# Moving the modulation column sums behind a step's products, and ordering the later modulation rows behind the convolutions and the gates

## The chip, the cores and the metric

One core of a Trainium2 chip runs the whole block. The metric is the device time of one execution in microseconds (us), smaller is better; the time given for a kernel is the median of its runs. The trace comes from one further, profiled execution.

## The reference

Input is x (1024 tokens by 1024 channels), a conditioning vector c and the weights of one layer. In outline:

```python
mod = silu(c) @ w_mod + b_mod                 # 6 rows of 1024
shift1, scale1, gate1, shift2, scale2, gate2 = split(mod, 6)
h = rms_norm(x, g_norm1) * (1 + scale1) + shift1
x_lru, z_lru, q, k, v = split(h @ w_in)       # 512 channels each
xc = conv4(x_lru) + conv_b                    # depthwise, 4 taps over the tokens
# per direction: r, i = sigmoid(xc @ w_a + b_a), sigmoid(xc @ w_x + b_x)
# a = exp(8 * r * log_sigmoid(lam)); u = sqrt(1 - a*a) * i * xc; h_t = a_t * h_{t-1} + u_t
y_lru = (h_fwd + h_bwd) * gelu(z_lru)
y_att = differential_attention(q, k, v)       # 4 heads, relative bias
x = x + gate1 * (concat(y_lru, y_att) @ w_out)
h2 = rms_norm(x, g_norm2) * (1 + scale2) + shift2
x = x + gate2 * expert_choice_ffn(h2)         # 16 experts, 128 tokens each
```

All matrices are float32. The kernel keeps that precision with split operands: a value is written as hi + lo in a short format, and a product is taken as hi*hi + hi*lo + lo*hi.

## The kernel before

**Stage 1, norm and first projection.** x is normalised, transposed (xT, 8 tiles of 128 channels by 1024 tokens) and turned into h. Tile k of h needs the 128 columns k of scale1 and shift1, so the modulation vector is made in slices: `m_load(k)` loads the weights of slice k in four DMAs, `m_mm(k)` multiplies their first four row blocks (of 8) on TensorE into `mp`, `m_sum(k)` adds the other four on VectorE (three instructions on `mp`, a fourth that writes `acc`), `m_red(k)` sums `acc` over the partitions with two matmuls against a column of ones into `pm`, and `m_col(k)` makes the two columns `acol` and `shc` on VectorE. `h_make(k)` then writes `hh` (ScalarE), the full-precision value (ScalarE again, or VectorE for k in 0, 1, 2, 7) and `hl`, their difference (GpSimd, VectorE for k = 7). `x_mm(k, lo, ms)` are the products of h tile k with the first 256 columns of w_in into the PSUM tiles `px[0]` and `px[1]` (the trace calls them `pjx`): `x_mm(k, False, (m,))` are 4 matmuls of `hh` into `px[m]`, `x_mm(k, True)` are 4 matmuls of `hl`. `w0_split` makes hi and lo of those weights, `lam_table` a small table for the gates.

In this stage the instruction order of TensorE, VectorE and ScalarE is the program's order (a `manual_schedule` block). GpSimd and the DMA queues are ordered by the planner. The loop over k makes slice k + 2 while the products of k and k - 1 run.

**Stage 2, the other projections.** q, k, v, z and the second half of x_lru go through TensorE in 256-column pieces; `do_x(ct, ps)` is the convolution of one 128-channel piece on VectorE (one instruction of line 451, three of line 453, out of PSUM), `do_lru(ct)` the gates (`pg` on TensorE, `tg` on ScalarE, lines 515 and 516 on VectorE, line 521 on GpSimd) and the two scans (lines 523 and 525). `proj_qk` squares and normalises q and k (`sqq`, `rq`, `nq`), transposes them (`pbq`, line 589) and splits them (line 596). Beside that the remaining four modulation rows (gate1, shift2, scale2, gate2) are made in two halves: `mod_rest(half, k)` loads two pieces of 128 x 1024 (`wr`, SyncE's DMA queue, into a ring of five `raw` buffers that the w_in pieces `wi` use too) and adds each to its sum `macc` with one VectorE instruction (line 620). `mod_out(half)` sums `macc` over the partitions on TensorE (`mq`).

In stage 2 a planner lays out every engine's instruction order when the program is built: by its own estimates of costs it takes, for each engine, the earliest instruction of the program that it thinks ready. Each engine then runs its list strictly in that order. `tc.issue_after(i)` keeps the instructions of the block behind i on i's engine. `mod_rest` uses it with the last entry of the list `behind`, to which `proj_qk` appends the instruction that writes `nq` or `nk`.

**After that** attention (about 320 to 556 us of the trace; TensorE, VectorE and ScalarE in program order), routing (556 to 604 us) and the 16 experts (604 to 1166 us), whose weights stream in from HBM.

Of the kernel before, what the change touches and what calls it, by code (L numbers as in the profile page):

```python
# [13 lines left out]
ALU = mybir.AluOpType  # L14
# [7 lines left out]
KT = D // P  # L22
# [34 lines left out]
KS = 3  # L57
KS0 = 1
KLT = 4
# [23 lines left out]
def tile_block(ctx: ExitStack, tc, x, cols, w_mod, b_mod, w_in, wa, wx, lam_qk, relT, w_out, g2, w_router,  # L83
# [68 lines left out]
    def load_in(c0, eng):  # L152
        return [load_half(c0, kk, eng) for kk in range(2)]
# [50 lines left out]
    def lam_table():  # L204
        V.tensor_scalar(out=e2, in0=e1, scalar1=2.0, scalar2=None, op0=ALU.add)
        V.reciprocal(out=e2, in_=e2)
        V.tensor_reduce(out=ls, in_=lp, op=ALU.add, axis=AX.X)
        act(ls, ls, AF.Exp)
        G_.tensor_tensor(out=nlam, in0=ls[:, 1:2], in1=ls[:, 0:1], op=ALU.subtract)
        G_.tensor_scalar(out=nlam, in0=nlam, scalar1=-LAM_INIT, scalar2=None, op0=ALU.add)  # L210
# [123 lines left out]
    def x_mm(k, lo, ms=(0, 1)):  # L334
        for m in ms:
            wh, wl = (w[:, k % 4, m * P:(m + 1) * P] for w in ws0[k // 4])
            for lt, h_ in ((wh, hl[k]),) if lo else ((wh, hh[k]), (wl, hh[k])):
                for n in range(2):
                    mm(px[m][:, n * 512:(n + 1) * 512], lt, h_[:, n * 512:(n + 1) * 512],
                       k == 0 and lt is wh and not lo, k == KT - 1 and lo)  # L340
# [9 lines left out]
    def w0_split(kk, part):  # L350
        if part == 0:
            ws0.append([ylp.tile([P, 4, 256], F32R, tag="y", bufs=NCT, name=f"w0{c}_{kk}") for c in "hl"])
            act(ws0[kk][0], w0r[kk])
        else:
            hi, lo = ws0[kk]
            V.tensor_tensor(out=lo, in0=w0r[kk], in1=hi.bitcast(F32), op=ALU.subtract)
# [14 lines left out]
    with tc.manual_schedule(engines={mybir.EngineType.PE, mybir.EngineType.DVE, mybir.EngineType.Activation}):  # L371
        c_silu()
        tables_a()
        act(rst[:, 0:1], epsc, AF.Sqrt)
        for t in range(NT + 1):
            if t < NT:
                x_stat(t)
            if 1 <= t <= NT:
                if t == NT:
                    m_mm(0)  # L380
                    m_sum(0)
                x_flip(t - 1)
                if t == NT:
                    m_red(0)
            if 2 <= t <= NT:
                x_evac(t - 2)
        w0_split(0, 0)
        m_col(0)
        x_evac(NT - 1, (0,))
        m_mm(1)  # L390
        warm(WU1)
        w0_split(0, 1)
        m_sum(1)
        h_make(0)
        m_red(1)
        m_col(1)
        x_evac(NT - 1, (1,))
        h_make(1)
        x_mm(0, False)
        m_mm(2)  # L400
        m_sum(2)
        x_mm(1, False, (0,))
        m_red(2)
        m_col(2)
        h_make(2)
        for k in range(1, KT + 1):
            if k + 3 < KT:
                m_load(k + 3)
            if k + 2 < KT:
                m_mm(k + 2)  # L410
                m_sum(k + 2)
            if k == 1:
                x_mm(0, True)
            elif k < KT:
                x_mm(k, False, (0,))
            if k + 2 < KT:
                m_red(k + 2)
                m_col(k + 2)
                i_act, i_pv = h_make(k + 2)
                if k + 2 < KT - 1:  # L420
                    i_pool = i_pv
                else:
                    i_dve = i_pv
            if k == KS:
                w0_split(1, 1)
            if k == KLT:
                lam_table()
            if k < KT:
                x_mm(k, False, (1,))
            if 1 < k < KT:  # L430
                x_mm(k - 1, True)
            if k == KS0:
                w0_split(1, 0)
            if k + 2 in (KW, KW + 1):
                wq0.append(load_half(1024, k + 2 - KW, V))
        x_mm(KT - 1, True)
# [11 lines left out]
    def do_x(ct, ps):  # L448
        cw = [col[:, C_CW + 4 * j + ct:C_CW + 4 * j + ct + 1] for j in range(4)]
        xc = lt_(f"xc{ct}")  # L450
        V.tensor_scalar(out=xc, in0=ps, scalar1=cw[2], scalar2=col[:, C_CB + ct:C_CB + ct + 1], op0=ALU.mult, op1=ALU.add)
        for j, o, i in ((0, slice(2, S), slice(0, S - 2)), (1, slice(1, S), slice(0, S - 1)), (3, slice(0, S - 1), slice(1, S))):
            last = V.scalar_tensor_tensor(out=xc[:, o], in0=ps[:, i], scalar=cw[j], in1=xc[:, o], op0=ALU.mult, op1=ALU.add)
        xc_[ct] = xc
        return last
# [21 lines left out]
    def proj_ch(ws, m, name, tag="pj"):  # L477
        ps = psb.tile([P, 1024], F32, tag=tag, bufs=2, name=name)
        for k in range(KT):
            wh, wl = (w[:, k % 4, m * P:(m + 1) * P] for w in ws[k // 4])  # L480
            for lt, hs in ((wh, (hh, hl)), (wl, (hh,))):
                for h_ in hs:
                    for n in range(2):
                        last = k == KT - 1 and lt is wl
                        mm(ps[:, n * 512:(n + 1) * 512], lt, h_[k][:, n * 512:(n + 1) * 512],
                           k == 0 and lt is wh and h_ is hh, last)
        return ps

    y_lru = []

    def do_lru(ct):
        xc = xc_[ct]
        xh = lt_(f"xch{ct}", None, F32R)
        xl = lt_(f"xcl{ct}", None, F32R)
        split(xc, xh, xl, V if ct in LV else G_)
        hs, st = [], []
        for d in range(2):
            pre = []
            for gi in range(2):
                pg = psb.tile([P, 1024], F32, tag="pg", bufs=2, name=f"pg{ct}_{d}_{gi}")  # L500
                i = d * 4 + ct
                for wi_, (w_, xv) in enumerate(((bdh, xh), (bdl, xh), (bdh, xl))):
                    for n in range(2):
                        mm(pg[:, n * 512:(n + 1) * 512], w_[gi][:, i, :], xv[:, n * 512:(n + 1) * 512], wi_ == 0, wi_ == 2)
                tg = lt_(f"tg{ct}_{d}_{gi}")
                act(tg, pg, AF.Tanh, scale=0.5, bias=hb[:, gi * 8 + i:gi * 8 + i + 1])
                pre.append(tg)
            ta, ti = pre
            i = d * 4 + ct
            tt = lt_(f"tt{ct}_{d}")  # L510
            act(tt, ta, AF.Tanh, scale=nkap[:, i:i + 1], bias=nkap[:, i:i + 1])
            act(ta, ta, AF.Exp, scale=kap[:, i:i + 1], bias=kap[:, i:i + 1])
            sq = lt_(f"sqa{ct}_{d}")
            act(sq, ta, AF.Square)
            V.scalar_tensor_tensor(out=tt, in0=sq, scalar=1.0, in1=tt, op0=ALU.add, op1=ALU.mult)
            V.scalar_tensor_tensor(out=ti, in0=ti, scalar=1.0, in1=xc, op0=ALU.add, op1=ALU.mult)
            st.append((ta, ti, tt))
        for d in range(2):
            ta, ti, tt = st[d]
            act(tt, tt, AF.Sqrt, scale=0.25)  # L520
            G_.tensor_tensor(out=ti, in0=ti, in1=tt, op=ALU.mult)
            if d == 0:
                V.tensor_tensor_scan(out=tt, data0=ta, data1=ti, initial=0.0, op0=ALU.mult, op1=ALU.add)
            else:
                V.tensor_tensor_scan(out=tt[:, ::-1], data0=ta[:, ::-1], data1=ti[:, ::-1], initial=0.0,
                                     op0=ALU.mult, op1=ALU.add)
            hs.append(tt)
        V.tensor_tensor(out=hs[0], in0=hs[0], in1=hs[1], op=ALU.add)
        hs_[ct] = hs[0]
# [84 lines left out]
    def mod_rest(half, *ks):  # L614
        for k in ks:
            for i in (2 * half, 2 * half + 1):
                w = raw_tile(f"wr{k}_{i}", [P, 1024])
                SY.dma_start(out=w, in_=w_mod[k * P:(k + 1) * P, (2 + i) * 1024:(3 + i) * 1024])
                with tc.issue_after(behind[-1].ins):
                    V.scalar_tensor_tensor(out=macc[i], in0=w, scalar=sc[:, k:k + 1], in1=macc[i], op0=ALU.mult, op1=ALU.add)  # L620
# [59 lines left out]
        V.tensor_scalar(out=s2w, in0=pw_[:, 0:NE], scalar1=-1.0, scalar2=None, op0=ALU.mult)  # L680

    wv0 = load_in(2048, G_)
    for m in range(2):
        do_x(2 + m, proj_ch(wx1, m, f"pjx1_{m}"))
    mod_rest(1, 2, 3)
    vt = [v_tile(f"v{h}", [P, NT, P]) for h in range(NH)]
    wz1 = load_in(768, V)
    mod_rest(1, 4)
    proj_v(wv0, 0, vt[0:2], lambda _: do_lru(2), VA)
    mod_rest(1, 5, 6)  # L690
    wv1 = load_in(2304, G_)
    do_lru(3)
    mod_rest(1, 7)
# [782 lines left out]
```

## Time and profile before

| | |
|---|---|
| median of 3 runs | 1175.16 us (1174.55, 1175.16, 1177.92) |
| profiled execution | 1174.46 us |
| its span, first to last instruction | 1172.7 us (1.76 us lie around it) |
| mean granted TensorE clock | 0.981 of full speed |
| TensorE busy | 1112.9 us, 95% of the span |
| VectorE, ScalarE, GpSimd busy | 956.9, 795.2, 452.8 us |

An engine's idle time counts for the result only where nothing else covers it. A row of a timeline gives start and duration in us, engine, line, operation, output<-inputs, shape and count of instructions merged into the row, and in brackets the engine's idle time just before it with what ended it. Line 93 is the helper that issues every matmul and line 90 the one that issues every ScalarE instruction, so those are told apart by their tiles.

### The profile page before, as it was taken

How to read it: one execution, taken by the hardware profiler on the slowest of the kernel's cores; microseconds unless marked ns; L12 is line 12 of the kernel's file. 1: busy time of each engine (PE TensorE's matmuls, PEld its weight loads, DVE VectorE, ACT ScalarE, POOL GpSimd, SP SyncE). 2: the span in 40 equal slices, each digit the busy share in tenths (PEclk: the TensorE clock that was granted, in tenths of full speed). 3: DMA queues.
4: the chain of work that ended last, by engine and by line, in shares of the span. 5: the costliest groups of instructions: out<-in, count | busy, mean ns of one | idle time of the engine just before them, and what ended most of it. 6: DMA issues, size and time to landing. Idle time of an engine off the chain costs nothing.

```text
span 1172.7 us, 17849 instructions
## 1 busy us (share of the span) xinstructions
PE 1112.9 (95%) x6303; PEld 933.0 (80%) x6303; DVE 956.9 (82%) x1258; ACT 795.2 (68%) x1051; POOL 452.8 (39%) x528
## 2 busy tenths in 40 slices
PE   5799999899999999999469999999999999999996
PEld 4599998788999998777348888888888888888885
DVE  7576757876498986645779999999999999999995
ACT  7439383186387887433438888888887787888784
POOL 4573332133134454444644323444332444332400
PEclk9899999999999999999779999999999999999998
DMA  9744646613683416336789999999999999999911
GB/s 329 221 126 142 225 135 216 233 55 80 179 246 114 112 37 214 137 127 216 285 326 334 372 394 383 393 389 401 387 394 391 365 391 410 394 392 390 389 39 18
DMA packets 146992, 304.33 MB, mean 260 GB/s; under 512 B 16972, under 2 KB 43724, under 8 KB 146900
## 3 DMA queue, kind: packets, MB, share of 16 engines
q1 hardware_dynamic: 135008, 279.99, 66.0%
q0 software_dynamic: 5488, 19.45, 6.3%
q10 hardware_dynamic: 6408, 3.77, 1.1%
q8 instruction: 49, 0.80, 0.3%
q14 instruction: 39, 0.32, 0.1%
HBM read 277.95 MB, written 25.21 MB: 259 GB/s over the span
## 4 chain that ended last, share of the span: by engine, by line
PE 84%; DVE 6%; DMA 4%; issue 3%; SPq 1%; ACT 1%; POOL 0%; POOLq 0%; DVEq 0%; ACTq 0%
PE ab L93 28%; PE y L93 14%; PE mix L93 7%; PE pv L93 5%; PE sc L93 5%; PE pjk L93 4%; PE pjq L93 3%; PE pjv L93 3%; PE pjz L93 3%; PE pw L815 2%; PE pg L93 2%; PE pjx L93 1%; PE pf L1360 1%; DMA wr<-in_w_mod_dram 1%; PE pe L1269 1%
## 5 line engine op out<-in xcount | busy, mean ns | idle before, releaser
L1260 POOL TENSOR_SCALAR oh<-iot,slot 128x128 bf16<-128x128 bf16 x120 | 143.8, 1213 | 252.6 <-PE pf L1360 238.5
L93 PE MATMUL ab<-wh,xeh 128*128 128x512 f32 x512 | 202.2, 395 | 0.2 <-ACT xeh L90 0.2
L93 PE MATMUL ab<-wh,xel 128*128 128x512 f32 x512 | 199.8, 390 | 0.1
L93 PE MATMUL ab<-wl,xeh 128*128 128x512 f32 x512 | 157.9, 390 | 0.0
L93 PEld LDWEIGHTS ab<-wl,xeh 128*128 128x128 f32 x512 | 96.2, 188 | 20.3
L93 PEld LDWEIGHTS ab<-wh,xel 128*128 128x128 f32 x512 | 96.3, 188 | 19.4 <-DVE xel L1273 0.5
L93 PEld LDWEIGHTS ab<-wh,xeh 128*128 128x128 f32 x512 | 96.1, 188 | 19.3 <-ACT xeh L90 0.5
L142 DVE TENSOR_TENSOR wl<-w_0r,wh 128x1024 fp32r<-128x1024 f32 x79 | 96.8, 1226 | 10.6 <-ACT wh L90 0.4
L90 ACT ACTIVATE wh<-w_0r 128x1024 fp32r<-128x1024 f32 x81 | 85.9, 1062 | 24.6 <-PE ab L93 14.9
L142 DVE TENSOR_TENSOR wl<-w_3r,wh 128x1024 fp32r<-128x1024 f32 x79 | 96.7, 1224 | 6.3
L90 ACT ACTIVATE wh<-w_1r 128x1024 fp32r<-128x1024 f32 x79 | 83.7, 1059 | 22.9 <-PE ab L93 18.2
L90 ACT ACTIVATE wh<-w_3r 128x1024 fp32r<-128x1024 f32 x79 | 83.9, 1062 | 22.3 <-PE ab L93 17.8
L142 DVE TENSOR_TENSOR wl<-w_2r,wh 128x1024 fp32r<-128x1024 f32 x80 | 96.4, 1221 | 2.3 <-ACT wh L90 0.3
L90 ACT ACTIVATE wh<-w_2r 128x1024 fp32r<-128x1024 f32 x80 | 84.9, 1061 | 19.6 <-PE ab L93 18.9
L142 DVE TENSOR_TENSOR wl<-w_1r,wh 128x1024 fp32r<-128x1024 f32 x78 | 92.6, 1220 | 3.6 <-ACT wh L90 1.6
L769 DVE CUSTOM_DVE_ANT_0 p<-sc,bias 128x1024 f32<-128x1024 f32 x64 | 77.8, 1218 | 10.9 <-PE sc L93 10.9
L93 PE MATMUL y<-wh,htl 128*128 128x512 f32 x256 | 83.0, 396 | 0.0
L93 PE MATMUL y<-wh,hth 128*128 128x512 f32 x256 | 81.1, 396 | 0.0
L93 PE MATMUL y<-wl,hth 128*128 128x512 f32 x256 | 79.6, 391 | 0.0
L90 ACT ACTIVATE p<-p,stat 128x1024 f32<-128x1024 f32 x60 | 68.4, 1150 | 0.3 <-DVE stat L769 0.3
L93 PEld LDWEIGHTS pv<-v,wt 128*128 128x128 f32 x512 | 61.7, 192 | 2.5
L93 PE MATMUL pv<-v,wt 128*128 128x128 f32 x512 | 62.1, 275 | 0.0
(466 smaller groups left out, 2832.1 us busy)
## 6 DMA issues: line engine op xcount, KB each, us to landing
w_0r<-in_w_dram SPq DMA_DIRECT2D x81, 512.0 KB, 6.8
w_1r<-in_w_dram SPq DMA_DIRECT2D x79, 512.0 KB, 8.4
w_2r<-in_w_dram SPq DMA_DIRECT2D x78, 512.0 KB, 9.3
w_3r<-in_w_dram SPq DMA_DIRECT2D x77, 512.0 KB, 9.2
wr<-in_w_mod_dram SPq DMA_DIRECT2D x32, 512.0 KB, 4.8
wi<-in_w_in_dram SPq DMA_DIRECT2D x18, 512.0 KB, 4.5
w_5r<-in_w_dram SPq DMA_DIRECT2D x17, 512.0 KB, 8.4
wm<-in_w_mod_dram SPq DMA_DIRECT2D x32, 256.0 KB, 4.9
```

What stands on the lines that cost most here:

```text
L90: return A.activation(out=out, in_=in_, func=func, **kw)
L93: return T.matmul(out, lhsT=lhsT, rhs=rhs, start=start, stop=stop)
L142: return (eng or V).tensor_tensor(out=lo, in0=src, in1=hi.bitcast(F32), op=ALU.subtract)
L769: V.tensor_tensor_reduce(out=p_, in0=scp[g, j], in1=prs[h][0][:, b0:b0 + S], op0=ALU.add, op1=ALU.min, scale=1.0, scalar=3.0e38, accum_out ...
L815: T.transpose(pw[:, b * P:(b + 1) * P], pt_[g, 0][:, kt * P:(kt + 1) * P], ident)
L1260: G_.tensor_scalar(out=oh[:, t, :], in0=iot, scalar1=slot[:, e, t:t + 1], scalar2=None, op0=ALU.is_equal)
L1269: T.transpose(pt[:, b * P:(b + 1) * P], xe[:, (kq * 4 + b) * P:(kq * 4 + b + 1) * P], ident)
L1360: T.transpose(pt[:, b * P:(b + 1) * P], sa[:, b * P:(b + 1) * P], ident)
```

## The change

First, in the loop of stage 1, the block with `m_red(k + 2)`, `m_col(k + 2)` and `h_make(k + 2)` moves from between the two halves of the `hh` products to behind all products of the step; `w0_split(1, 1)` (one VectorE instruction, at k = 3) and `lam_table()` (at k = 4) now stand in front of it. Second, `do_x` and the gate instruction of line 516 leave handles, and the `behind` list gets new last entries, so that the second half's row 4 is queued behind the convolution of piece 2, row 5 behind the convolution of piece 3, and rows 6 and 7 behind the last gate instruction of line 516 in `do_lru(2)`. Rows 0 to 3 stay behind the last `nk`.

```diff
@@ stage 1, loop over k
             elif k < KT:
                 x_mm(k, False, (0,))
+            if k == KS:
+                w0_split(1, 1)
+            if k == KLT:
+                lam_table()
+            if k < KT:
+                x_mm(k, False, (1,))
+            if 1 < k < KT:
+                x_mm(k - 1, True)
             if k + 2 < KT:
                 m_red(k + 2)
                 m_col(k + 2)
...
-            if k == KS:
-                w0_split(1, 1)
-            if k == KLT:
-                lam_table()
-            if k < KT:
-                x_mm(k, False, (1,))
-            if 1 < k < KT:
-                x_mm(k - 1, True)
@@ do_lru
-            V.scalar_tensor_tensor(out=ti, in0=ti, scalar=1.0, in1=xc, op0=ALU.add, op1=ALU.mult)
+            tis.append(V.scalar_tensor_tensor(out=ti, in0=ti, scalar=1.0, in1=xc, op0=ALU.add, op1=ALU.mult))
@@ stage 2
+    convs = []
     for m in range(2):
-        do_x(2 + m, proj_ch(wx1, m, f"pjx1_{m}"))
+        convs.append(do_x(2 + m, proj_ch(wx1, m, f"pjx1_{m}")))
     mod_rest(1, 2, 3)
+    behind.append(convs[0])
     vt = [v_tile(f"v{h}", [P, NT, P]) for h in range(NH)]
     wz1 = load_in(768, V)
     mod_rest(1, 4)
+    behind.append(convs[1])
     proj_v(wv0, 0, vt[0:2], lambda _: do_lru(2), VA)
-    mod_rest(1, 5, 6)
+    mod_rest(1, 5)
+    behind.append(tis[-1])
+    mod_rest(1, 6)
     wv1 = load_in(2304, G_)
     do_lru(3)
     mod_rest(1, 7)
```

## Rows read from the trace of the kernel before

**Rows 1.** The page's first part: busy time, share of the span and instructions of each engine.

```profile
PE 1112.9 (95%) x6303; PEld 933.0 (80%) x6303; DVE 956.9 (82%) x1258; ACT 795.2 (68%) x1051; POOL 452.8 (39%) x528
```

**Rows 2.** Busy time by stretch (start:end and length, then busy us and instructions of PE, PEld, DVE, ACT, POOL, then granted clock, DMA share and GB/s): stage 1 and the experts.

```profile
0.00:66.00 66.00, 48.02 (x281) 34.25 (x282) 41.09 (x86) 38.63 (x58) 37.38 (x89) 0.95 0.83 265
...
604.00:1166.00 562.00, 558.59 (x2672) 457.08 (x2672) 532.95 (x540) 447.60 (x478) 201.34 (x149) 1.00 0.95 352
```

**Rows 3.** What TensorE waited for from 0 to 330 us: us in total, times, longest.

```profile
PE pm L93 <- DVE acc L305: 6.5, 6, 1.6
PE pg L93 <- DVE lk L596: 2.3, 1, 2.3
...
PE pjv L93 <- DVE xc L453: 1.7, 1, 1.7
```

**Rows 4.** TensorE's timeline in stage 1, from the sum of slice 2 to that of slice 6.

```profile
30.39 0.61 PE L93 MATMUL pm<-ones,acc 128*128 128x1 f32 x4 [1.54 <-DVE acc L305]
...
34.32 0.61 PE L93 MATMUL pm<-ones,acc 128*128 128x1 f32 x4 [1.63 <-DVE acc L305]
34.79 0.70 PE L93 MATMUL pjx<-hh,w0h 128*128 128x512 f32 x2
...
35.89 0.85 PE L93 MATMUL mp<-wm,scz 128*32 128x256 f32 x8
36.67 1.22 PE L93 MATMUL pjx<-hh,w0h 128*128 128x512 f32 x2
...
38.90 1.01 PE L93 MATMUL pm<-ones,acc 128*128 128x1 f32 x4 [0.16 <-DVE acc L305]
...
43.28 0.64 PE L93 MATMUL mp<-wm,scz 128*32 128x256 f32 x8
...
46.11 0.61 PE L93 MATMUL pm<-ones,acc 128*128 128x1 f32 x4 [1.04 <-DVE acc L305]
46.57 0.72 PE L93 MATMUL pjx<-hh,w0h 128*128 128x512 f32 x2
...
47.60 1.09 PE L93 MATMUL pjx<-hl,w0h 128*128 128x512 f32 x4
48.61 0.64 PE L93 MATMUL mp<-wm,scz 128*32 128x256 f32 x8
...
51.43 0.61 PE L93 MATMUL pm<-ones,acc 128*128 128x1 f32 x4 [1.05 <-DVE acc L305]
```

**Rows 5.** Busy time by stretch again (columns as in rows 2), for two stretches of stage 1; the figure after the busy times is the granted clock.

```profile
37.00:40.00 3.00, 2.84 (x9) 1.93 (x9) 1.79 (x5) 1.75 (x2) 2.12 (x1) 0.50 1.13 333
...
43.40:57.00 13.60, 10.46 (x63) 6.38 (x61) 7.99 (x20) 6.46 (x6) 6.21 (x3) 1.00 0.44 133
```

**Rows 6.** Timelines of VectorE, ScalarE and GpSimd in stage 1: the sum of slice 5, the weight split, and the tile that `h_make(6)` makes.

```profile
43.99 1.54 DVE L305 SCALAR_TENSOR_TENSOR mp<-wm,sc,mp 128x256 f32<-128x256 f32 x3 [3.76 <-PE mp L93]
45.57 0.48 DVE L305 SCALAR_TENSOR_TENSOR acc<-wm,sc,mp 128x256 f32<-128x256 f32 x1
...
46.95 1.22 DVE L356 TENSOR_TENSOR w0l<-w,w0h 128x1024 fp32r<-128x1024 f32 x1
...
52.40 1.24 ACT L90 ACTIVATE hh<-xT,shc,acol 128x1024 fp32r<-128x1024 f32 x1 [2.81 <-DVE shc L317]
53.67 1.24 ACT L90 ACTIVATE xT<-xT,shc,acol 128x1024 f32<-128x1024 f32 x1
...
54.99 2.36 POOL L329 TENSOR_TENSOR hl<-xT,hh 128x1024 fp32r<-128x1024 f32 x1 [2.96 <-ACT xT L90]
```

**Rows 7.** Timelines of ScalarE, VectorE and TensorE around the first transpose of stage 2.

```profile
80.31 1.06 ACT L90 ACTIVATE bdh<-bd 128x1024 fp32r<-128x1024 f32 x1 [1.26 <-DMA bd<-in_wx_dram]
81.27 1.01 ACT L90 ACTIVATE sqq<-pjq 128x1024 f32<-128x1024 f32 x1
...
84.29 1.23 DVE L582 TENSOR_TENSOR nq<-pjq,rq 128x1024 f32<-128x1024 f32 x1
...
85.66 1.04 PE L589 MATMUL pbq<-ident,nq 128*128 128x128 f32 x8
```

**Rows 8.** Timelines of GpSimd and VectorE around the convolutions of pieces 2 and 3 and the first scan of `do_lru(2)`.

```profile
217.68 2.40 POOL L142 TENSOR_TENSOR wi_1l<-wi,wi_1h 128x1024 fp32r<-128x1024 f32 x1 [11.92 <-ACT wi_1h L90]
...
216.00 1.28 DVE L620 SCALAR_TENSOR_TENSOR macc<-wr,sc,macc 128x1024 f32<-128x1024 f32 x1 [3.11 <-DMA wr<-in_w_mod_dram]
...
218.40 2.77 DVE L620 SCALAR_TENSOR_TENSOR macc<-wr,sc,macc 128x1024 f32<-128x1024 f32 x1
...
233.27 1.27 DVE L596 SCALAR_TENSOR_TENSOR lk<-pbk,gqk,hk 128x1024 fp32r<-128x1024 f32 x1
...
250.22 2.29 DVE L523 TENSOR_TENSOR_SCAN tt<-tg,tg 128x1024 f32<-128x1024 f32 x1 [4.76 <-POOL tg L521]
```

**Rows 9.** All instructions on the modulation sums `macc`: count, shortest/median/longest in ns, and when the first and the last started.

```profile
L620 DVE SCALAR_TENSOR_TENSOR macc<-wr,sc,macc x32: 1267/1278/3266, 75.0 to 241.0; 128x1024 f32<-128x1024 f32 x32
...
L93 PE MATMUL mq<-macc,ones x16: 592/604/617, 188.2 to 270.6; 128*32 128x512 f32 x16
```

**Rows 10.** DMA issues from 0 to 330 us: queue, count, size of one, median us from issue to landing.

```profile
wr<-in_w_mod_dram SPq DMA_DIRECT2D x32, 512.0 KB, 4.8
...
wm<-in_w_mod_dram SPq DMA_DIRECT2D x32, 256.0 KB, 4.9
```

**Rows 11.** SyncE's DMA queue: the issues of the weights of slices 4 to 7, first to last merged.

```profile
26.14 13.64 SPq L288 DMA_DIRECT2D wm<-in_w_mod_dram  x16
```

More of the change, by code (lines that the diff above doesn't have):

```diff
@@ L487, in proj_ch @@
         return ps
-    y_lru = []
+    y_lru, tis = [], []
     def do_lru(ct):
```

## Prediction

> **What bounds the kernel now.** I read the page first. TensorE is busy for 95% of the span [rows 1], so time comes off only where TensorE stands idle or runs at a lower clock. Busy time by stretch says where that is: 48.0 of 66 us in stage 1, against 558.6 of 562 us in the experts [rows 2]. The list of TensorE's waits in the first 330 us names what it stood for: 6.5 us in six waits for `acc`, the modulation sum that VectorE hands to `m_red`, then 2.3 us behind `lk` and 1.7 us behind a convolution [rows 3]. The timeline shows the six waits one by one, each in front of a `pm` matmul [rows 4], and a second granted-clock table shows one more loss: from about 37 us the clock is at 0.50, the lower of its two levels (1.2 instead of 2.4 GHz), and by 43.4 it is back at 1.00 [rows 5]. The clock fell after TensorE had stood idle for 1.54 and then 1.63 us [rows 4].
>
> All sums below go against the profiled execution, 1174.46 us (span 1172.7). The median of the runs shown stands 0.7 above it, and I add that at the end. A difference under 0.3%, 3.5 us, can't be told from no change.
>
> **Part one: `m_red` behind the step's products.** Nothing is added or removed; the same matmuls stand in another order. So the gain is what the waits and the low clock cost.
>
> *Slice 3 (k = 1).* The wait is 1.63 us. The four products from 34.79 to 35.89, 1.10 us, now run in it [rows 4]. VectorE's sum is no earlier, so 0.53 us of wait is left: gain 1.10.
>
> *Slices 4 to 7 (k = 2 to 5).* Twelve matmuls now stand between `m_mm` and `m_red`. Four take 1.03 us (46.57 to 47.60) or 1.01 (47.60 to 48.61) [rows 4], so together about 3.07. VectorE's sum takes 2.06 (43.99 to 45.57 + 0.48) [rows 6]. It is hidden with 1.0 to spare, and the waits of 0.16, 1.04 and 1.05 go, and with them the one for slice 7, about 1.1 (the 6.5 less the five shown). That is 3.3; the first wait of 1.54, for slice 2, stands ahead of the loop and stays [rows 3, 4].
>
> *The clock.* From 36.67 to 43.28 TensorE did twelve products and one `pm` in 6.61 us, 0.16 of it idle [rows 4]. At the high level the same takes 1.03 + 1.03 + 1.01 + 0.46 (`pm`, 46.11 to 46.57) = 3.5, so 2.9 was lost, and 0.2 more on the `mp` group at 35.89 (0.85 against 0.64): 3.1. Does the fall go away? Bounds: 0 and 3.1. It fell behind idle times of 1.54 and 1.63 us; from 43.4 to 57 it stays at 1.00 with single waits of about 1.05 [rows 4, 5]. After the change 1.54 and 0.53 are left, which is neither case. I take 3.1, since the product groups move into the very wait that the fall came behind, and keep 0 as a rival.
>
> *What becomes late.* `h_make(k + 2)` comes three product groups later within the step. For slice 6 `m_red` began at 51.43 [rows 4], `hh` was written from 52.40 to 53.64 and `hl` by 57.35 [rows 6], so 2.2 and 5.9 us behind `m_red`. The first product that reads `hh` stands a whole step later: about 0.46 + 0.57 + 3.07 + 0.46 + 0.57 = 5.1 us (0.57 for an `mp` group: its 0.64 [rows 4] less the overlap with the next). Spare: 2.9; for `hl`, used one step later still, over 5. `w0_split(1, 1)`, 1.22 us [rows 6], and `lam_table`'s small instructions now fall into VectorE's spare microsecond and the 0.46 of `m_red`; if they overrun, they eat from the 2.9. ScalarE is idle for 2.81 us in front of `h_make` [rows 6], which covers the table load that comes forward. Cost: nothing. The weight DMAs hold too: the last of slices 4 to 7 is issued at 39.78 and lands 4.9 us later, about 44.7 [rows 10, 11], while the last `m_mm` would come near 47.1 (34.8 plus three steps of 0.46 + 0.57 + 3.07).
>
> *What follows it into stage 2.* By this sum TensorE ends stage 1 earlier by 1.10 + 3.3 + 3.1 = 7.5 us. Not everything moves with it. `m_red(6)` moves from 51.43 [rows 4] to 34.32 + 3 x 4.1 = 46.6 (a step is 0.46 + 0.57 + 3.07), by 4.8 only, since two product groups that stood behind it now stand in front. GpSimd's `hl` of slice 6 follows it, then the gate tables, the zeroing of the gate weights' tiles and their DMAs, and at last ScalarE's `bdh`, behind which `sqq` is queued; `sqq` leads through `nq` (ends 85.52) to the transposes at 85.66 [rows 7]. There is 0.1 us of spare, so if the order stays, TensorE waits there for the difference: 7.5 - 4.8 - 0.1 = 2.6. If the planner now puts `sqq` in front of `bdh`, the loss is 0. I take 2.6, since the row shows the order as it is. Part one: 7.5 - 2.6 = 4.9.
>
> **Part two: rows 4 to 7 behind convolutions and gates.** No instruction is added. On VectorE a row-4 instruction stood in front of the convolution's second step and held it while its own DMA was in flight: 3.11 us idle, then 1.28; the next took 2.77 [rows 8]. The convolution of piece 2 therefore ended late, its PSUM tile came free late, and TensorE's first `pjv` waited 1.7. Row 5 and 6 instructions then pushed `lk` to 233.27, whose PSUM tile the gates needed: 2.3 [rows 3, 8]. With the rows behind the convolutions, that of piece 2 ends at least 3.11 + 1.28 + 2.77 = 7.2 us earlier, more than the waits behind it, and both should go: 4.0. Bounds: 0, where something else holds the same two tiles, and 4.0. The row instructions behind the waits are the cause named, so I take 4.0.
>
> What is late next: rows 6 and 7, four instructions of 1.28 [rows 9], come after the gates. VectorE is idle for 4.76 us in front of the scan at 250.22 [rows 8], which covers them. Their `raw` buffers come free later, so row 7's two DMAs are issued later on SyncE's queue, behind them on that queue the first loads of attention. The last `macc` instruction began at 241.0, and the `mq` matmuls that read it run at 270 [rows 9]: some 27 us of room for one DMA of 4.8 [rows 10] and 5 us of VectorE.
>
> **Sum.** 1174.46 - 1.10 - 3.3 - 3.1 + 2.6 - 1.7 - 2.3 = 1165.6; with the 0.7 for the median, 1166.3. Attention, routing and experts should only shift: they start when stage 2's tiles are there, and their loads follow their own buffers.
>
> **Rivals.**
>
> *The clock falls all the same.* The 1.54 us wait remains and 0.53 behind it. For: it is the same pair of waits that came before the fall [rows 4]. Against: two thirds of the second are filled. 3.1 less: 1169.4. Chance 0.22.
>
> *GpSimd and VectorE hold each other up.* The `macc` instruction at 218.40 took 2.77 instead of 1.28 while GpSimd ran a 2.40 us subtraction from 217.68; it ended 1.09 after GpSimd did [rows 8]; the longest took 3.27 [rows 9]. Rows 6 and 7 now meet GpSimd's 2.4 us products and splits of `do_lru(2)` and `(3)`. Four times 3.27 - 1.28 is 8 us, of which the 4.76 idle covers a part; the 3 us beyond it and GpSimd's own delay can reach TensorE's gates. Then part two's 4.0 is lost and up to 2 more: 1170.3 to 1172.3, say 1171. Chance 0.12. This is what the Trainium skill states (SBUF — State Buffer, section "SBUF: two separate sides"): a VectorE instruction with two SBUF inputs and a GpSimd instruction that reads SBUF contend for one shared port pair, whoever starts first holds it for the whole instruction, and the other blocks. By that rule the trace agrees, 1.49 us late at 218.40, and these four moved rows are the ones exposed.
>
> *The planner's new order brings new waits.* Stage 2 isn't ordered by hand, and a stage 1 that is shorter by some us changes what it thinks ready. Waits of 1.7 to 2.3 us are what such misplacements cost here [rows 3]; three or four new ones give back 7: 1173. Chance 0.10.
>
> *Slower: row 7 holds VectorE.* If row 7's instructions are queued ahead of the scans, each stands for its DMA as at 216.00: 4.8 + 1.3 us, twice, 12 us, and scans, gates and `mq` behind it stand too. It decides once TensorE loses more than the 8.9 gained and 3.5 beyond; with all 12 and a further stall of 3 or more at `mq`: 1181. Against: the 27 us of room. Chance 0.06.
>
> **How the numbers follow.** Forecast 0.50, the rivals 0.22, 0.12, 0.10 and 0.06. The likeliest case by itself spans 1163.7 (no wait at the transposes) to 1168. Below 1161.5 would need both that and a further wait removed; above 1172.5 lie the last rival and half of the one before. Range 1161.5 to 1172.5. Faster by over 0.3% (below 1171.6) takes in the forecast, the first rival and two thirds of the second: 0.80. Slower (above 1178.7): 0.07, the last rival and a worse case of the third. Same: 0.13.
>
> **What would show it.** Right: the four waits of `pm` for `acc` in the loop gone and one near 0.5 left; the clock at 1.00 through 34 to 45 us; stage 1's last `pjx` 7 us earlier; the first `pbq` waiting about 2.6; no wait of `pjv` for `xc` or of `pg` for `lk`, no VectorE idle behind a `wr` DMA inside a convolution. Wrong: a low clock after the first wait, `macc` instructions above 2 us beside GpSimd near the scans, VectorE idle for a `wr` DMA behind the gates, or waits of TensorE in stage 2 under names that the rows here don't have.

## The result, and the profile after

The changed kernel takes 1164.78 us (median of 6 runs, 1162.60 to 1167.24) against 1175.16 (6 runs, 1171.86 to 1178.21): a ratio of 0.9909, interval 0.9886 to 0.9931. Its profiled execution is the longest of its six, 1167.24 us (span 1165.5, mean granted clock 0.978), so the rows below go against that time and not against the median. A second profiled execution of the same kernel took 1163.18 us (span 1161.5, 0.982); it stands among the experiments as `e11_change`.

The page's first part and the busy time by stretch (columns as in rows 2; the experts now start 7.4 us earlier):

```profile
PE 1113.3 (96%) x6303; PEld 935.2 (80%) x6303; DVE 960.6 (82%) x1258; ACT 795.1 (68%) x1051; POOL 457.9 (39%) x528
```

```profile
0.00:66.00 66.00, 52.35 (x321) 40.54 (x321) 47.14 (x89) 38.54 (x58) 40.23 (x87) 0.92 0.85 272
596.70:1158.70 562.00, 558.54 (x2672) 456.70 (x2672) 533.21 (x540) 447.65 (x477) 202.19 (x149) 1.00 0.95 352
```

TensorE is busy for 52.4 instead of 48.0 us of the first 66 [rows 2]. Of what is left idle there, 11.3 us are waits for the first tiles of x; before it was 11.2, a line that stands above those quoted in [rows 3], and the change doesn't touch it. The experts are the same to 0.05 us. They only shifted: their first matmul started at 604.11 before and starts at 596.75 now, the last one at 1162.36 and 1154.94.

What TensorE waited for from 25 to 330 us (us in total, times, longest):

```profile
PE pg L93 <- ACT tg L90: 2.2, 1, 2.2
PE pm L93 <- DVE acc L305: 2.0, 2, 1.5
PE pbk L589 <- DVE nk L582: 1.2, 1, 1.2
```

Against [rows 3]: the six waits for `acc` are two, and the waits for `lk` and for the convolution are gone. The first line isn't new: it was 1.7 before, below the lines quoted in [rows 3], and is now 2.2. No wait of `pbq` is there.

TensorE's timeline in stage 1, to be laid beside [rows 4]:

```profile
30.25 0.61 PE L93 MATMUL pm<-ones,acc 128*128 128x1 f32 x4 [1.53 <-DVE acc L305]
...
35.03 1.01 PE L93 MATMUL pm<-ones,acc 128*128 128x1 f32 x4 [0.46 <-DVE acc L305]
...
42.27 0.52 PE L93 MATMUL pm<-ones,acc 128*128 128x1 f32 x4
...
46.17 0.50 PE L93 MATMUL pm<-ones,acc 128*128 128x1 f32 x4
...
50.03 0.50 PE L93 MATMUL pm<-ones,acc 128*128 128x1 f32 x4
```

Slices 4 to 7 have no wait. Full-clock steps are 3.86 to 3.90 us long (42.27, 46.17, 50.03), against 5.32 before (46.11 to 51.43, [rows 4]). The step from 35.03 to 42.27 is 7.24: TensorE runs at the lower clock there, as the busy time by stretch shows (the 0.50 behind the busy times is the granted clock).

```profile
28.00:32.00 4.00, 2.47 (x19) 1.47 (x18) 3.16 (x8) 0.78 (x1) 2.33 (x2) 1.00 1.07 322
32.00:42.30 10.30, 9.84 (x32) 6.75 (x31) 5.10 (x11) 3.89 (x4) 5.20 (x3) 0.50 1.13 342
...
253.60:257.40 3.80, 3.73 (x9) 2.94 (x10) 3.80 (x3) 3.73 (x5) 1.00 (x1) 0.55 0.02 4
```

So the clock fell for 10.3 us in stage 1, longer than the 6 to 7 us of before [rows 4, 5], and once more near 254, behind the 2.2 us wait of `pg`.

To compare kernels I use two lengths from TensorE's timeline. **Stage 1** runs from the start of the last matmul of `pt` (the transposes of x) to the first `pjq`, **stage 2** from there to the first `sc` of attention. The clock is the mean granted one of the stretches 28 to 45 us and 230 to 262 us. One profiled execution each:

| kernel | median us | ratio to before, interval | stage 1 | stage 2 | clock 28–45 | clock 230–262 |
|---|---|---|---|---|---|---|
| before | 1175.16 | | 43.37 | 237.41 | 0.80 | 1.00 |
| the change | 1164.78 | 0.9909 (0.9886–0.9931) | 38.72 | 234.99 | 0.70 | 0.95 |
| e11_change, again | 1163.72 | 0.9901 (0.9885–0.9918) | 35.45 | 233.40 | 0.90 | 1.00 |
| e1_stage1_only | 1166.28 | 0.9936 (0.9921–0.9952) | 35.02 | 237.44 | 1.00 | 1.00 |
| e2_rows_only | 1171.45 | 0.9979 (0.9969–0.9990) | 43.73 | 233.40 | 0.80 | 1.00 |
| e3_fill | 1163.42 | 0.9910 (0.9894–0.9925) | 35.50 | 233.40 | 1.00 | 1.00 |
| e4_before_fill | 1174.02 | 0.9990 (0.9981–1.0000) | 42.46 | 238.73 | 1.00 | 0.95 |
| e5_kh | 1161.73 | 0.9888 (0.9869–0.9908) | 33.52 | 233.44 | 1.00 | 1.00 |
| e6_lv | 1163.47 | 0.9905 (0.9885–0.9924) | 34.89 | 232.76 | 1.00 | 1.00 |
| e7_no_gates | 1164.18 | 0.9902 (0.9882–0.9921) | 37.05 | 232.88 | 0.90 | 1.00 |
| e8_conv0_only | 1164.38 | 0.9906 (0.9885–0.9927) | 38.72 | 235.09 | 0.70 | 0.95 |
| e9_kh_lv | 1162.43 | 0.9886 (0.9870–0.9903) | 33.50 | 234.31 | 1.00 | 0.95 |
| e10_kh_lv_nogates | 1159.32 | 0.9862 (0.9846–0.9879) | 33.49 | 231.14 | 1.00 | 1.00 |

The two stages account for the profiled difference: 4.65 + 2.42 = 7.1 of 1174.46 - 1167.24 = 7.2 us. In the second profiled execution they give 7.92 + 4.01 = 11.9, from which 0.7 goes because its last `pt` started that much later (22.84 instead of 22.14): 11.2 of 11.3.

### The profile page after: what moved, and what is told of

Read it like the earlier page. It is cut to its first block, busy times and chain, and to the rows that moved or that the text cites. A ratio compares the mean times of both kernels' runs of the same rounds, so it can differ in the third digit from the quotient of the medians.

```text
span 1165.5 us, 17852 instructions
## 1 busy us (share of the span) xinstructions
PE 1113.3 (96%) x6303; PEld 935.2 (80%) x6303; DVE 960.6 (82%) x1258; ACT 795.1 (68%) x1051; POOL 457.9 (39%) x528
## 4 chain that ended last, share of the span: by engine, by line
PE 88%; DVE 4%; issue 3%; SPq 2%; DMA 1%; ACT 1%; POOLq 0%; POOL 0%; DVEq 0%; ACTq 0%
PE ab L93 28%; PE y L93 14%; PE mix L93 7%; PE pv L93 5%; PE sc L93 5%; PE pjk L93 4%; PE pjv L93 4%; PE pjz L93 4%; PE pjx L93 4%; PE pjq L93 3%; PE pw L820 2%; PE pg L93 2%; SPq L288 1%; PE pf L1365 1%; PE pe L1274 1%
```

## The experiments

**Each part alone.** `e1_stage1_only` has the new loop and the old order of the rows; `e2_rows_only` the old loop and the new order. Against the changed kernel and the kernel before:

```diff
@@ e1_stage1_only, from the changed kernel
-    behind.append(convs[0])
-    behind.append(convs[1])
-    behind.append(tis[-1])
@@ e2_rows_only, from the kernel before
+    behind.append(convs[0])
+    behind.append(convs[1])
+    behind.append(tis[-1])
```

> Only the first part of the change (column sums behind the step's products); rows 4 to 7 as in the kernel before. If the waits count one by one: 4.4 us of waits gone, 0 to 3.1 for the clock, so 1167.7 to 1170.8 against 1175.2; the waits of pjv for the convolution (1.7) and of pg for lk (2.3) still there. Rival, a shift that stage 2 takes back at its first transposes (2.6 us): 1170 to 1173, with a wait in front of pbq.

> Only the second part (rows 4 to 7 behind convolutions and gates); stage 1 as in the kernel before. If the waits count one by one: the waits of 1.7 and 2.3 gone, 4.0 us, so 1171.2; if the row instructions that now stand among the scans cost the gates as much, 1173 to 1175. The six waits for acc in stage 1 (6.5 us) remain. If the two parts add up, the gains of the two runs come to the 10.4 us of the whole change.

TensorE's waits in `e1_stage1_only` (columns as above), and the two `pm` rows of its timeline:

```profile
PE pm L93 <- DVE acc L305: 2.7, 2, 1.5
PE pg L93 <- DVE lk L596: 2.4, 1, 2.4
PE pg L93 <- ACT tg L90: 1.7, 1, 1.7
PE pjv L93 <- DVE xc L453: 1.7, 1, 1.7
```

```profile
30.98 0.61 PE L93 MATMUL pm<-ones,acc 128*128 128x1 f32 x4 [1.54 <-DVE acc L305]
...
35.36 0.61 PE L93 MATMUL pm<-ones,acc 128*128 128x1 f32 x4 [1.16 <-DVE acc L305]
```

The first part alone leaves both waits of stage 2 and takes 8.35 us off stage 1 (43.37 to 35.02) in an execution whose clock didn't fall. Its median of 1166.28 lies 1.4 below the range that I expected for it. There is no wait at `pbq`, with the rows in their old order too. The second part alone takes 4.0 off stage 2 (237.41 to 233.40) and leaves stage 1 within 0.4 us of what it was (43.73 against 43.37), though its waits for `acc` came to 7.9 us instead of 6.5. The parts add up: 0.64% and 0.21% by the ratios, 0.85%, against 0.91% and 0.99% for the whole.

**Is it the idle time that lets the clock fall?** `e3_fill` and `e4_before_fill` put products that nobody reads in front of `m_red`, so that TensorE works through the wait: 6 and 2 of them in front of slices 2 and 3 of the changed kernel; 6, 7, none, 4, 4 and 4 in front of slices 2 to 7 of the kernel before. The edit of `e3_fill`; `e4_before_fill` has other counts:

```diff
+    def fill(n, name):
+        if n:
+            dm = psb.tile([P, 512], F32, tag="pg", bufs=2, name=f"fill{name}")
+            for _ in range(n):
+                mm(dm, ws0[0][0][:, 0, 0:P], hh[0][:, 0:512], True, True)
...
+        fill(6, 2)
         m_red(2)
...
+                fill({1: 2}.get(k, 0), k + 2)
                 m_red(k + 2)
```

> The whole change, and in stage 1's two remaining waits for acc six and two extra 512-column products into a PSUM tile that nobody reads. If the clock falls because TensorE stands idle in these waits: granted clock 1.00 from 28 to 43 us in the profile, and 3.4 to 5.1 us of low clock saved against a run in which it falls, so 1160 to 1162. Rival, a fall that has nothing to do with those waits: the clock still at 0.50 somewhere in 30 to 43 us and 1164.8 as the change itself.

> The kernel before, with the waits of 1.54, 1.63, 1.04, 1.05 and 1.05 us filled with 6, 7, 4, 4 and 4 such products. The waits cost what they cost before, only as busy time; so the time moves by the clock term alone: 1172 (3.1 less) if the fall goes away, 1175 if it does not, and up to 1 us more where the extra products delay the sums.

In both the granted clock stayed at 1.00 from 28 to 45 us, and neither got faster for it: `e3_fill` 1163.42, above the 1160 to 1162 that I expected and not to be told from the change; `e4_before_fill` 1174.02, a ratio of 0.9990, where I expected 1172. In the first, the wait in front of slice 3 was 1.14 us in spite of its fillers:

```profile
30.65 0.58 PE L93 MATMUL pm<-ones,acc 128*128 128x1 f32 x4 [0.26 <-DVE acc L305]
...
35.45 0.58 PE L93 MATMUL pm<-ones,acc 128*128 128x1 f32 x4 [1.14 <-DVE acc L305]
```

In the second, idle time was turned into work (6.5 us of waits became 3.0) that nobody needed, and a 3.4 us stretch of low clock came later, from 234.3 to 237.7:

```profile
234.30:237.70 3.40, 3.25 (x8) 2.57 (x9) 3.40 (x4) 0.28 (x1) 0.00 (x0) 0.51 0.87 321
```

So fillers don't pay. Whether they keep the clock up, one execution of each can't show: `e1_stage1_only` and `e6_lv` run the changed kernel's stage 1 without them and were at 1.00 as well. The thirteen profiled executions together point that way. In eight of them slice 2 waited its full 1.53 to 1.54 us, and in six of the eight the clock fell in stage 1; in the five in which that wait was filled or shorter (0.26 in the two filled ones, 1.05 to 1.06 in `e5_kh`, `e9_kh_lv` and `e10_kh_lv_nogates` below) it fell in none.

**What holds slice 3?** With the clock up, `pm` of slice 3 waits 1.0 to 1.6 us in kernels with the new loop. VectorE's and GpSimd's timelines show why, before (first two lines) and in the changed kernel (last two). `h` is VectorE's full-precision copy, `hl` GpSimd's subtraction:

```profile
31.36 0.94 DVE L326 TENSOR_SCALAR h<-xT,acol,shc 128x1024 f32<-128x1024 f32 x1
...
31.72 5.14 POOL L329 TENSOR_TENSOR hl<-h,hh 128x1024 fp32r<-128x1024 f32 x2
```

```profile
31.22 1.79 DVE L326 TENSOR_SCALAR h<-xT,acol,shc 128x1024 f32<-128x1024 f32 x1
...
30.08 2.37 POOL L329 TENSOR_TENSOR hl<-h,hh 128x1024 fp32r<-128x1024 f32 x1
```

In the profiled execution of the kernel before, VectorE's copy started (31.36) ahead of `hl` and took 0.94. In that of the change GpSimd's `hl` starts first, at 30.08, and ends at 32.45; the copy, begun at 31.22, ends at 33.01, 0.56 behind it. The same copy takes 0.81 where GpSimd is idle. The sum of slice 3 is queued behind the copy.

But it isn't the change that reversed the two. `e2_rows_only` has the old loop, and there GpSimd comes first as well: the copy takes 1.73, and the wait of slice 3 is 2.13 instead of 1.63. On GpSimd a small instruction stands in front of `hl`, `lp` of line 370. In the kernel before it waited for its DMA until 31.30, just ahead of the copy (first line); in `e2_rows_only` it ran 1.60 us ahead of the copy (the other three lines: GpSimd, VectorE, TensorE):

```profile
31.30 0.46 POOL L370 TENSOR_TENSOR lp<-lq 128x128 f32<-128x128 f32 x1 [3.48 <-DMA lq<-in_lam_qk_dram]
...
30.56 0.46 POOL L370 TENSOR_TENSOR lp<-lq 128x128 f32<-128x128 f32 x1 [1.94 <-DMA lq<-in_lam_qk_dram]
...
32.16 1.73 DVE L326 TENSOR_SCALAR h<-xT,acol,shc 128x1024 f32<-128x1024 f32 x1
...
35.91 1.01 PE L93 MATMUL pm<-ones,acc 128*128 128x1 f32 x4 [2.13 <-DVE acc L305]
```

In all nine other profiled executions with this copy on VectorE, old loop or new, `lp` starts 1.4 to 2.1 us ahead of the copy and the copy takes 1.26 to 1.91. The profiled execution that the prediction was read from is the exception. `e5_kh` gives this copy and the one before it to ScalarE, which in the changed kernel was idle for 4.54 us in front of its `hh` at 31.22:

```diff
-KH = (0, 1, 2, 7)
+KH = (0, 7)
```

> The whole change, and the full-precision h tiles of k = 1 and 2 written by ScalarE instead of VectorE. If stage 1's last two waits (1.53 in front of slice 2's sum, 0.46 to 1.16 in front of slice 3's) are VectorE's, held by GpSimd's subtraction of hl on the way (its copy took 2.19 and 1.79 instead of 0.81): the second wait gone, the first near 1.0, 1.5 us less than the change: 1163. Rival, waits that come from the modulation weights' DMAs or from ScalarE instead: no wait shorter, 1165.

```profile
30.50 0.61 PE L93 MATMUL pm<-ones,acc 128*128 128x1 f32 x4 [1.06 <-DVE acc L305]
33.86 0.61 PE L93 MATMUL pm<-ones,acc 128*128 128x1 f32 x4
```

TensorE's timeline: the first wait falls from 1.54 to 1.06, the second, on slice 3, is gone from the list. Stage 1 takes 33.52 us, 1.5 less than `e1_stage1_only`, and the median is 1.7 to 2.7 below those of the three kernels run beside it with the change's stage 1 (`e6_lv`, `e7_no_gates`, `e8_conv0_only`). So the cause of the wait is the copy in front of the sum, not the length of the sum. The run takes away the copy's own 0.81 together with what GpSimd adds to it (0.98 in the change, 0.59 in `e1_stage1_only`), so it doesn't tell the two apart; the durations say that the hold is about half of it. The Trainium skill (SBUF — State Buffer, section "SBUF: two separate sides") states that VectorE in its two-port mode and GpSimd lock one port pair for a whole instruction; with 1.79 instead of 0.81, and an end that follows GpSimd's by 0.56, the trace agrees, though no row says in which mode the copy runs.

**The wait of `pg` for `tg`.** It grew from 1.67 us before to 2.22. VectorE's line 515 behind the first scan of `do_lru(2)` before (first line), and VectorE and GpSimd there in the changed kernel:

```profile
253.01 3.24 DVE L515 SCALAR_TENSOR_TENSOR tt<-sqa,tt 128x1024 f32<-128x1024 f32 x1
...
243.12 1.26 DVE L620 SCALAR_TENSOR_TENSOR macc<-wr,sc,macc 128x1024 f32<-128x1024 f32 x1
...
244.90 2.82 DVE L515 SCALAR_TENSOR_TENSOR tt<-sqa,tt 128x1024 f32<-128x1024 f32 x1
...
243.45 3.18 POOL L142 TENSOR_TENSOR xcl<-xc,xch 128x1024 fp32r<-128x1024 f32 x1 [2.58 <-issue]
```

An instruction of row 7 runs when GpSimd starts on `xcl`, which takes 3.18 instead of the 2.40 it took before and takes in `e7_no_gates`. `xcl` in turn holds line 515, which takes 1.22 where nothing holds it; that isn't new (3.24 before, 2.82 now), but line 515 ends 4.52 us behind the scan instead of 3.74. Three runs take this apart: `e6_lv` makes `xcl` of piece 3 on VectorE; `e7_no_gates` leaves rows 6 and 7 behind the convolution of piece 3; `e8_conv0_only` puts all four rows behind that of piece 2.

```diff
@@ e6_lv
-LV = ()
+LV = (3,)
@@ e7_no_gates; e8_conv0_only takes out both lines
-    behind.append(tis[-1])
@@ e8_conv0_only
-    behind.append(convs[1])
```

> The whole change, and the lo part of the last convolution's split (xcl of piece 3) on VectorE instead of GpSimd. The change left a wait of 2.22 us of pg for tg near 253. If it comes from GpSimd holding VectorE up (the gate instruction at 244.90 took 2.82 instead of 1.2 beside that split): 1 to 1.6 us of the wait gone, 1163.5. Rival, a wait set by ScalarE's own queue or by row 7's instruction ahead of the gate instruction: the wait within 0.5 us of 2.2, 1165.

> The whole change without its last step: rows 6 and 7 are queued behind the convolution of piece 3 like row 5, not behind the gates. If the order behind the convolutions is what brought the gain: the waits of pjv and of pg for lk stay away and the later pg wait goes back from 2.2 to about 1.7, so 1164.3 (0.5 less). If rows 6 and 7 must stand behind the gates: a wait of TensorE for the gates of piece 2 that the change does not have, 1166 or more.

> The whole change, but of the row orders only the first: rows 4 to 7 all behind the convolution of piece 2. If the two waits that went have two causes: the 1.7 of pjv stays away and the 2.3 of pg for lk is back, because rows 5 and 6 stand in front of the convolution of piece 3 and of lk again: 1167. Rival, one cause for both: both away, 1165.

`e7_no_gates`: the wait is back at 1.68 and stage 2 is 0.5 shorter (232.88); `xcl` takes 2.40. The order behind the gates isn't what the gain comes from; in the profiled executions it costs half a microsecond. `e6_lv`: the wait falls to 0.62 and stage 2 by 0.64 only, since GpSimd's next product meets the row and split instructions of VectorE and takes 4.54 instead of 2.40, and a new wait of 0.74 at `ps2w` follows:

```profile
244.34 4.54 POOL L521 TENSOR_TENSOR tg<-tg,tt 128x1024 f32<-128x1024 f32 x1 [6.41 <-ACT tt L90]
...
255.59 1.96 PE L93 MATMUL ps2w<-wr,s2c 128*128 128x16 f32 x16 [0.74 <-ACT tg L90]
```

`e8_conv0_only`: neither the wait of `pjv` nor that of `pg` for `lk` comes back, though instructions of rows 5 to 7 again stand in front of gate instructions and three of them wait for their DMAs (VectorE's timeline, the longest of the three waits):

```profile
224.96 1.27 DVE L596 SCALAR_TENSOR_TENSOR lk<-pbk,gqk,hk 128x1024 fp32r<-128x1024 f32 x1
...
234.97 1.28 DVE L620 SCALAR_TENSOR_TENSOR macc<-wr,sc,macc 128x1024 f32<-128x1024 f32 x1 [1.64 <-DMA wr<-in_w_mod_dram]
```

`lk` comes at 224.96, not at 233.27 as before [rows 8]. So the first new entry alone, which queues all four rows behind the convolution of piece 2, removes both waits. The planner put only one instruction of rows 5 and 6 in front of `lk` here, against three before, so the run by itself doesn't clear these rows. The distance from the convolution's end does. Before (first line) and in the changed kernel:

```profile
223.47 1.27 DVE L453 SCALAR_TENSOR_TENSOR xc<-pjx,col,xc 128x1023 f32<-128x1023 f32 x1
...
221.19 1.27 DVE L596 SCALAR_TENSOR_TENSOR lk<-pbk,gqk,hk 128x1024 fp32r<-128x1024 f32 x1
```

Before, `lk` (233.27) followed the convolution's end (224.74) by 8.5 us. In the changed kernel it follows it (212.03) by 9.2, in `e8_conv0_only` (213.19) by 11.8, both without the wait. `e8_conv0_only` drew the long fall of the clock in its profiled execution, 0.70 and 0.95, like the first of the change; its stages, 38.72 and 235.09, are those of the change to 0.1 us. Its wait of `pg` for `tg` is 2.32 all the same, and not from `xcl`, which takes 2.40 here. From the first `pjq` to the first scan of `do_lru(2)` it takes 180.84 us, against 180.18 in the change and 180.19 in `e7_no_gates`: row 7's two waits for its DMAs (2.0 us) now stand in front of the gates.

**Both moves together, and the change once more.** `e9_kh_lv` has the edits of `e5_kh` and `e6_lv`, `e10_kh_lv_nogates` also that of `e7_no_gates`.

> The change with both moves off VectorE's blocked instructions: h of k = 1, 2 by ScalarE (e5, 3.0 us faster than the change by medians) and the LRU piece 3's copy on VectorE (e6, 0.64 us in stage 2). If the two are independent, stage 1 stays at e5's 33.5 and stage 2 falls from 33.4's level of 233.4 to 232.8: 1161.1 us. Rival: the gain of 0.6 goes into the new wait of the softmax tile that e6 showed, or e5's lead was in part its clock (no fall in its profiled run): 1161.7 to 1163.5.

> The same without the last order (rows 6 and 7 behind the convolution of piece 3, not behind the gates). If the order behind the gates costs 0.5 us, as e7's wait suggested (1.68 instead of 2.22), 0.5 less than e9 in stage 2: 1160.6. Rival: with piece 3's copy on VectorE the wait at the gates was already down to 0.62, so there is nothing left to gain: the same as e9; or rows 6 and 7 now fall between the copy and the gates and hold them: 1 to 2 more than e9.

> The change itself, on the same chip and in the same rounds as the two above, with a profile of its own. Theory (the fall of the clock in stage 1 is drawn anew at each execution and is not removed): 1162.6 to 1167.3 over its runs, stage 1 at 35.0 where the clock does not fall and 37 to 38.8 where it does, whichever this profiled run draws. Rival (the fall belongs to the order of the instructions): 10 us of low clock behind the first wait again, as in the first profile of the change.

`e9_kh_lv` can't be told from `e5_kh` by the ratios (0.9886 and 0.9888), and its stage 2 is 0.9 longer (234.31): what moving `xcl` gains is lost again, to waits of 0.62 and 0.73 and a stretch of low clock behind them. Without row instructions between the gates, `e10_kh_lv_nogates` has neither wait; GpSimd's product is back at 2.42, and stage 2 takes 231.14. What TensorE still waits for:

```profile
PE pbk L589 <- DVE nk L582: 1.2, 1, 1.2
PE pm L93 <- DVE acc L305: 1.1, 1, 1.1
PE pw L819 <- DVE p L812: 0.4, 1, 0.4
```

At 1159.32 us (1158.65 to 1159.64) it beats the change (1163.18 to 1164.58 beside it) and the kernel before. I had expected 0.5 from this edit and it gave 3.1: the two waits (1.35) and, in the profiled execution, the low clock behind them (3.4 us at 0.50, some 1.6).

`e11_change` drew a short fall, from 31.8 to 35.2 us, behind the first wait:

```profile
31.80:35.20 3.40, 3.40 (x14) 2.15 (x7) 3.29 (x6) 1.24 (x1) 2.71 (x2) 0.50 0.98 279
```

The same program, first 0.70 and then 0.90: where and how long the clock falls differs from execution to execution. It isn't settled what decides it in one execution; the runs show only that in stage 1 the wait of 1.5 us was followed by a fall in six executions of eight.

## Why the prediction was right, and where its steps were not

**The four waits of slices 4 to 7: right, and worth more.** They are gone. I priced them at their idle time, 1.05 each. The step went from 5.32 to 3.86 us, 1.46, so 0.41 more than the wait. Of this, 0.16 is the overlap between one matmul's end and the next one's start, which a stopped TensorE loses at the last product (49.76 + 0.46 against 50.38, the end of its 0.62). The other 0.25 lies in groups that have other neighbours now: from start to start the `hl` products take 0.92 instead of 1.01, the `hh` products that stood behind `pm` 0.46 instead of 0.56. Why they are shorter is not shown. The 1.46 holds for the steps at the full clock, two of the four in the profiled execution before; in the two steps with the fall, the waits and the clock together gave 4.0 (11.79 against 7.83 in `e1_stage1_only`), 0.3 less than I had for them.

**Slice 3: 0.53 forecast, 0 to 1.61 found.** The step that failed is the 1.63 it started from, with "VectorE's sum is no earlier". The sum is later in every other profiled execution with this copy on VectorE, with the old loop too (2.13 in `e2_rows_only`), because GpSimd's subtraction starts before VectorE's copy and holds it; 2.13 less the 1.10 would have given 1.03. At the high clock the wait is 1.0 to 1.6 (`e1`, `e6_lv`, `e7_no_gates`); at the low one the products in front take longer and hide it, 0.46 in the first profile and none in `e11_change`.

**The clock: this step failed.** I took 3.1 us for a fall that would go away. It did not: 10.3 us at 0.50 in the first profiled execution, 3.4 in the second, none in `e1` and `e6_lv`. It seems to be a draw in the kernel before as well: its 41 runs beside these kernels go from 1172.5 us (mean clock 0.983) to 1177.7 (0.977), though where in the run the clock fell is known only for the profiled one. With the same stage 1 the long fall costs 3.7 us (38.72 against 35.02). In the change's profiled execution it was longer than in that of before; this is the first rival, "the clock falls all the same".

**The new wait at `pbq`, 2.6: not there.** I took the order of before, with the zeroing of the gate weights' tiles late. The planner now puts that zeroing in front of most of the tables: GpSimd did it at 63.35 instead of 72.00 (first line, before), and `nq` started at 75.67 and ended at 76.90, 4 us before the first `pbq` at 80.88.

```profile
72.00 1.85 POOL L467 MEMSET bd<- 128x1024 f32 x2
...
63.35 1.86 POOL L467 MEMSET bd<- 128x1024 f32 x2
...
75.67 1.23 DVE L582 TENSOR_TENSOR nq<-pjq,rq 128x1024 f32<-128x1024 f32 x1
```

**`h_make` later, loads, table load: right.** No wait of `pjx` for `hh` or `hl`, none for a weight DMA.

**Part two: 4.0 forecast, 4.0 found** (237.41 to 233.40 in `e2`, `e3` and `e11`), less 1.6 where the clock falls behind `pg`. The convolution of piece 2 runs through in VectorE's timeline:

```profile
206.73 1.34 DVE L451 TENSOR_SCALAR xc<-pjx,col 128x1024 f32<-128x1024 f32 x1
208.11 3.92 DVE L453 SCALAR_TENSOR_TENSOR xc<-pjx,col,xc 128x1022 f32<-128x1022 f32 x3
211.94 4.61 DVE L620 SCALAR_TENSOR_TENSOR macc<-wr,sc,macc 128x1024 f32<-128x1024 f32 x2
```

But the two waits have one cause, not two: `lk` was late because the convolution was (8.5 us behind its end before, 9.2 now), not because rows 5 and 6 pushed it further.

**The other rivals.** GpSimd and VectorE do hold each other up, but at the gates for 0.55 us and not for 4 to 6; in stage 1, where I hadn't looked for it, it lengthens slice 3's copy by 0.45 to 1.10, with the old loop as with the new. The planner's order brought no new wait. Row 7 didn't hold VectorE in the change; in `e8_conv0_only`, where it stands in front of the gates, it did by some 0.65.

**The sum.** The direction and the two groups of waits came as argued; that the number came out only 1.5 us above the median is in part luck. Against the profiled execution I had 8.9: 7.5 from stage 1 and 4.0 from the rows, less 2.6 at `pbq`. The change's first profiled execution gave 4.65 + 2.42: the clock that went on falling took 2.9 from the first term and 1.6 from the second, and the 2.6 that wasn't there made up for most of it. The second gave 7.92 + 4.01, so there the missing 2.6 is the main error. My estimate for an execution without a fall is 1162.7 (the 1163.18 of `e11_change` less the 0.4 of its fall); the fastest one seen is 1162.60.

## What to carry to other kernels

Price a stopped engine by the distance between two equal points of its loop, not by the idle time alone. Where VectorE and GpSimd share a stage, look which starts first, and in more than one execution: here a GpSimd instruction that waited for its DMA one or two microseconds longer in one execution turned the two round, and the other engine's instruction took 0.94 instead of up to 1.91. Giving that copy to an idle engine (here ScalarE) took another 1.5 us off the stage. A loss that is drawn anew at each execution, as the low clock is here, doesn't belong in a sum as a term that an edit removes; give it as a spread, and take it from several executions.

## What the runs showed of the hardware that was not expected

- The granted clock of one and the same program from 28 to 45 us was 0.70 in one execution and 0.90 in another, and 1.00 for two kernels with the same stage 1; it fell behind waits of 1.5 us with TensorE at work between them. The Trainium skill (TensorE: Matmul & The Clock Gate, section "What's actually happening") says that the window in which the activity is watched runs freely and isn't reset when the kernel starts, so that the point of a change varies. The point varies here too (1.8 us behind the start of slice 2's `pm` in the change, 0.7 in `e11_change`); that this is the reason, and why a fall lasted 10.3 us, 3.4 or didn't come, no run shows.
- A low clock can be nearly free: 3.4 us of it cost 0.4 in `e11_change` (35.45 against 35.02), where it took the place of the 1.16 us wait of slice 3, and 1.6 in stage 2, where no wait stood behind it (234.99 against 233.40). In `e7_no_gates` 3.4 us of it came behind that wait, from 37.2 to 40.6, and stage 1 took 37.05.
- VectorE's held copy ends 0.54 to 0.57 us behind GpSimd's subtraction in nine executions (33.01 against 32.45 in the change), whatever its length; line 515, which has two tile inputs, ends 1.08 to 1.09 behind `xcl` (256.25 against 255.17 before, 247.72 against 246.63 in the change). Both are less than the same instruction takes alone (0.81 and 1.22), so it looks as if most of the work, but not all, comes after GpSimd's end.
